# A hybrid decoder step: row values of a gated recurrence spread over partitions by transfers through DRAM, in place of matrix products

## The chip, the core and the metric

The kernel runs on one core of one Trainium2 chip, as one program. The core has a matrix engine (PE, with its weight loads shown as PEld), a vector engine (DVE), an activation engine (ACT), a general engine (POOL) and a sync engine (SP), which here issues every transfer. Each engine works through its own instructions in order; semaphores make an engine wait for another or for a transfer. The metric is the device time of one execution in microseconds, lower is better, taken as the median over runs.

## What is computed

One inference step of one layer. 16 meta tokens and 2048 prompt tokens (16 chunks of 128), and 32 sample tokens (8 sequences of 4), go through a layer norm and one input projection of width 3848. Half of the width feeds an mLSTM group (4 heads of 128, a recurrence with a running maximum), half a sliding-window attention with sinks; gates, one output projection and a second layer norm follow. The part that the change touches is the mLSTM of a chunk:

```python
b = jnp.cumsum(log_f, axis=1)
dmat = b[:, :, None, :] - b[:, None, :, :] + log_i[:, None, :, :]
inter = b + m[:, None, :]
m_t = jnp.maximum(inter, jnp.max(dmat, axis=2))
w = jnp.exp(dmat - m_t[:, :, None, :])
s_inter = jnp.exp(inter - m_t)
qk = jnp.einsum('bthd,bshd->btsh', q, k) * w
num = jnp.einsum('btsh,bshd->bthd', qk, v) + jnp.einsum('bthk,bhkv->bthv', q, c) * s_inter[..., None]
den = jnp.sum(qk, axis=2) + jnp.einsum('bthk,bhk->bth', q, n) * s_inter
h = num / jnp.maximum(jnp.abs(den), jnp.exp(-m_t))[..., None]
c_new = decay[..., None, None] * c + jnp.einsum('bsh,bshk,bshv->bhkv', w_state, k, v)
n_new = decay[..., None] * n + jnp.einsum('bsh,bshk->bhk', w_state, k)
```

The sample tokens go through the same formulas, with a state c, n, m for each of 8 sequences and 4 heads.

## The kernel before, in words

The program has a start (weights staged, scaled and split into two float16 parts, the meta and sample tokens projected) and then two long phases.

**Phase A** takes the 16 prompt chunks through the mLSTM. `a_steps(n)` is a generator whose steps are, for chunk n: the gate projection (`a_gate`), the projections q, k, v, o (`a_proj(n, 0..3)`, 24 matrix products of 128x512 each, lines 296 to 299), `m_rows(n)` (the gates are transposed so that a head is a row and time runs along it; two scans give the decay rows and the running maximum), `m_weights(n)` (the rows are brought back to one value per token and head, and the decay weights `wt` and `SI` are made), `m_S(n)` (q times k), and for the chunk before `m_num(n - 1)` and `m_kv(n - 1)`. The last two steps load x for chunk n + 2 and normalise it (`norm_x`). Between these steps a second generator, `jobs()`, is advanced: the sample tokens' mLSTM (`d_prepare`, then `d_head` for each head), the preparation of six later weights (kv, aq, az, z, o0, o1), and the sample's attention. `pace(0.8)` advances it at 8 of 10 steps.

The point that the change is about: the row M (running maximum less its own decay sum) lies on one partition per head, and the weights need it on all 128 partitions. Before, `m_weights` makes this spread with PE: `sel[:, h]` has ones in the row of head h, and four float32 products of 128x128 (line 762, two passes each) put M, spread over the partitions, in a PSUM tile from the pool `pt` (three tiles, which the transposes, the gates and the scores also use). DVE and ACT then read it there (lines 772, 776, 778). `d_prepare` does the same for the sample tokens (line 656), and in `d_head` the state C is multiplied by q in 8 products of 128 columns (line 702), each followed by one of a single column for the normaliser n (line 703).

Prepared weights are kept in a pool `wp` of five tiles. Four hold w_q, w_k, w_v, w_o through phase A; the fifth is used by one prepared weight after another, each written to DRAM (`spill`, 2 MB) before the next takes its tile, and fetched again (`reload`) when phase A leaves the tiles free.

**Phase B** takes the 16 chunks through the attention, the gates and the output projection: per chunk `b_q`, `b_kv`, `b_az`, `b_z` on PE, the score units `s_unit`, `s_pv`, and for the chunk before `b_out` (two products with wr_o, the second layer norm, the store).

A scheduler decides the order on every engine from the order of the source, the dependences and the tiles of the pools; it lets the mLSTM of a chunk run beside the projections of the next one. All transfers are issued by SP through `dma` (line 103 of the kernel before) in one order, and an issue that has to wait holds up those behind it.

## Time and profile before

| | |
|---|---|
| three runs | 1099.37, 1101.61, 1102.27 us; median 1101.61 us |
| the profiled execution | 1096.6 us, of which the span from first to last instruction is 1094.8 us |
| mean granted PE clock in it | 0.984 of full speed |
| start, until the first chunk is through its projections | about the first 110 us |
| phase A | about 110 to 560 us |
| phase B with the tail | about 560 us to the end |

A profile page gives busy times per engine, a strip of 40 slices of the span, the chain of work that ended last, and the costliest groups of instructions. Times inside the span are counted from its first instruction.

### The profile page before, as it was taken

To read this page: it belongs to the slowest core of one execution; us is meant where nothing else is said; L and a number is where in the kernel's file an instruction comes from. 1 tells how busy PE (TensorE), PEld (TensorE's weight loads), DVE (VectorE), ACT (ScalarE), POOL (GpSimd) and SP (SyncE) were. 2 spreads that over 40 slices of the span, in tenths; PEclk is the share of its full clock that TensorE was granted. 3 is DMA by queue.
4 is the path that set the end of the run, shared out by engine and by line. 5 is a ranking of instruction groups with operands and counts; after the bars stand their busy time and mean duration, and the time that the engine had idled before them with its cause. 6 is when DMAs were issued, how large, how long until landed. Compare 5 with 4: busy or idle time off the path is not lost.

```text
span 1094.8 us, 17806 instructions
## 1 busy us (share of the span) xinstructions
PE 1039.4 (95%) x6455; PEld 577.1 (53%) x6455; DVE 735.2 (67%) x2069; ACT 443.3 (40%) x1108; POOL 262.9 (24%) x270
## 2 busy tenths in 40 slices
PE   7969999999989999889998999999999999999986
PEld 3425565565556555445564554555555555555543
DVE  6769676776766777866655676566666656667664
ACT  5646333235434344562225344343344333344430
POOL 2113232121111111101311332233332233332222
PEclk9989999999999999999999999999999999999998
DMA  9746545445974568478585555656555464544552
GB/s 321 197 129 174 148 129 119 109 119 135 292 171 124 127 218 240 131 224 288 206 280 101 117 115 131 127 119 120 127 94 134 123 139 115 123 105 108 109 106 76
DMA packets 246098, 166.04 MB, mean 152 GB/s; under 512 B 207977, under 2 KB 220985, under 8 KB 244441
## 3 DMA queue, kind: packets, MB, share of 16 engines
q1 hardware_dynamic: 246010, 164.90, 58.9%
q8 instruction: 51, 0.84, 0.3%
q14 instruction: 37, 0.30, 0.1%
HBM read 70.32 MB, written 45.68 MB: 106 GB/s over the span
## 4 chain that ended last, share of the span: by engine, by line
PE 59%; DMA 15%; DVE 13%; ACT 6%; issue 5%; POOL 2%; SPq 1%; DVEq 0%; ACTq 0%; POOLq 0%
PE pj L1339 14%; PE pj L297 11%; PE pj L296 11%; PE pj L299 11%; DMA xT<-hl 3%; PE pt L1259 2%; DMA EE<-stg 2%; PE po L1312 2%; DMA stg<-in_dram 2%; DVE xs L380 1%; DMA stg<-hl 1%; DMA wd_z<-w_z 1%; DMA wd_o<-w_o 1%; ACT hl L321 1%; PE po L826 1%
## 5 line engine op out<-in xcount | busy, mean ns | idle before, releaser
L1339 PE MATMUL pj<-wr_o,EE 128*128 128x512 f16 x720 | 166.9, 381 | 3.0 <-DMA EE<-stg 1.5
L296 PEld LDWEIGHTS <-xT 128*128 128x128 f16 x992 | 97.9, 99 | 103.1 <-issue 6.9
L297 PEld LDWEIGHTS <-xT 128*128 128x128 f16 x992 | 97.8, 99 | 97.3 <-issue 6.8
L299 PEld LDWEIGHTS <-xT 128*128 128x128 f16 x992 | 96.8, 98 | 97.8
L1339 PEld LDWEIGHTS <-EE 128*128 128x128 f16 x720 | 70.5, 98 | 81.1 <-DMA EE<-stg 3.4
L325 POOL TENSOR_TENSOR lns<-lns,mhalf 128x1 f32<-128x1 f32 (+1 forms) x16 | 21.3, 1332 | 175.5 <-ACT lns L324 158.7
L1268 DVE TENSOR_TENSOR hl<-g,hl 128x512 f16<-128x512 f32 (+1 forms) x32 | 23.2, 724 | 49.1 <-ACT hl L1267 49.1
L1272 POOL TENSOR_TENSOR mhl<-g,mhl 128x32 f16<-128x32 f32 x32 | 18.8, 587 | 145.1 <-ACT mhl L1271 145.1
L296 PE MATMUL pj<-w_q,xT 128*128 128x512 f16 x120 | 47.1, 392 | 6.0 <-DMA xT<-hl 6.0
L1272 POOL TENSOR_TENSOR mhl<-SI,mhl 128x32 f16<-128x32 f32 x32 | 18.5, 578 | 139.1 <-ACT mhl L1271 139.1
L1266 ACT ACTIVATE g<-g,nb 128x272 f32<-128x272 f32 (+1 forms) x64 | 32.4, 507 | 46.3 <-DVE nb L1263 46.3
L296 PE MATMUL pj<-wr_z,xT 128*128 128x512 f16 x128 | 48.8, 381 | 0.0
L297 PE MATMUL pj<-wr_z,xT 128*128 128x512 f16 x128 | 48.7, 380 | 0.0
L296 PE MATMUL pj<-w_v,xT 128*128 128x512 f16 x120 | 46.3, 386 | 2.4 <-DVE q L431 2.4
L296 PE MATMUL pj<-wr_az,xT 128*128 128x512 f16 x128 | 48.5, 379 | 0.0
L296 PE MATMUL pj<-wr_aq,xT 128*128 128x512 f16 x128 | 48.5, 379 | 0.0
L297 PE MATMUL pj<-wr_aq,xT 128*128 128x512 f16 x128 | 48.5, 379 | 0.0
L297 PE MATMUL pj<-wr_az,xT 128*128 128x512 f16 x128 | 48.5, 379 | 0.0
L787 POOL TENSOR_TENSOR qs<-qs,SI 128x512 f32<-128x512 f32 x16 | 23.8, 1486 | 98.2 <-ACT SI L778 98.1
L297 PE MATMUL pj<-w_q,xT 128*128 128x512 f16 x120 | 47.0, 392 | 0.0
L297 PE MATMUL pj<-w_v,xT 128*128 128x512 f16 x120 | 46.5, 388 | 0.0
L297 PE MATMUL pj<-w_o,xT 128*128 128x512 f16 x120 | 46.5, 388 | 0.0
(459 smaller groups left out, 2510.4 us busy)
## 6 DMA issues: line engine op xcount, KB each, us to landing
stg<-in_dram SPq DMA_DIRECT2D x28, 512.0 KB
xs<-in_dram SPq DMA_DIRECT2D x16, 512.0 KB
h_d<-xs SPq DMA_DIRECT2D x16, 512.0 KB
xT_d<-xT SPq DMA_DIRECT2D x16, 512.0 KB
xs<-h_d SPq DMA_DIRECT2D x16, 512.0 KB
xT<-xT_d SPq DMA_DIRECT2D x16, 512.0 KB
out_dram<-xs SPq DMA_DIRECT2D x15, 512.0 KB
hn_d<-g SPq DMA_DIRECT2D x16, 258.0 KB
```

The lines of the kernel that those rows point to most:

```text
L296: T.matmul(ps, xT[:, k, :], w.t[:, k, 0, :n], start=(k == 0), stop=False)
L297: T.matmul(ps, xT[:, k, :], w.t[:, k, 1, :n], start=False, stop=False)
L299: T.matmul(ps, xT[:, KT + k, :], w.t[:, k, 0, :n], start=False, stop=(k == KT - 1))
L321: A.activation(junk[:, 0:D], x, AF.Copy, accum_out=sm)
L325: G.tensor_tensor(rs, ve, mhalf[:rows, 0:1], op=ALU.pow)
L787: G.tensor_tensor(c.qs, c.qs, c.SI, op=ALU.mult)
L1259: T.matmul(ps[:, lo:], c.qT[:, h], kTs[:, 2 * (h // 4) + x, lo:], start=(x == 0), stop=(x == 1))
L1266: A.activation(p[:, i, lo:], p[:, i, lo:], AF.Exp, bias=nb[:, h:h + 1], accum_out=sums[:, h:h + 1])
L1268: V.tensor_tensor(hl[:, 1, 2 * q:2 * q + 2, lo:], p[:, :, lo:2 * P], hl[:, 0, 2 * q:2 * q + 2, lo:], op=ALU.subtract)
L1272: G.tensor_tensor(m[:, 1], p[:, :, 2 * P:], m[:, 0], op=ALU.subtract)
L1312: T.matmul(pso[:, h], l, r, start=False, stop=(i == len(last) - 1), skip_group_check=True)
L1339: T.matmul(ps, c.yT[:, a, :], w[:, k, t, :], start=(first and j == 0), stop=(last and j == len(mm) - 1))
```

## The change

1. `sel` and its products go. `m_rows` writes each head's row of M to DRAM (four transfers of 512 bytes from one partition each) and reads the four rows back into an SBUF tile `Mb` on all 128 partitions (one transfer, 128 x 2 KB, the same 2 KB read for every partition). DVE and ACT read `Mb` there.
2. `a_gate(n + 1)` and `m_rows(n + 1)` are called in chunk n, around `a_proj(n, 3)`.
3. `d_prepare` does the same for the sample's row, with one more step of the generator.
4. In `d_head` the sample's normaliser becomes column 128 of C: 8 products of 129 columns in place of 8 of 128 and 8 of 1; the decay and the update go over 129 columns, and the separate instructions on n go; one DVE copy per head puts n in, one ACT copy takes it out.
5. x of chunk n + 3 is loaded before chunk n + 2 is normalised. The steps of a chunk are 9 instead of 10, and `pace(.92)` advances the other generator at 92 of 100 of them.
6. w_o1 is not spilled and reloaded: its tile is kept, so that the reload of aq has to wait for a tile of the projection weights. `b_out(0)` moves from chunk 1 of phase B to chunk 2, ahead of the score units.

The core of the diff:

```diff
-    sel = cst.tile([P, H, P], F32, name="sel")
-    G.memset(sel, 0.0)
-    for h in range(H):
-        G.memset(sel[32 * h:32 * h + 1, h], 1.0)
...
+    m_d = [dr.tile([H, P], F32, name=f"m_d{n}") for n in range(NCH)]
+    m5_d = dr.tile([H, 40], F32, name="m5_d")
...
-        ps = pt([P, H, 40])
         for h in range(H):
-            T.matmul(ps[:, h], sel[:, h], M5, start=True, stop=True)
-        A.activation(Mb5.rearrange("p h b s -> p (h b s)"), ps.rearrange("p h t -> p (h t)"), AF.Copy)
+            dma(m5_d[h:h + 1], M5[32 * h:32 * h + 1])
+        dma(Mb5.rearrange("p h b s -> p (h b s)"), m5_d.rearrange("(o h) t -> o (h t)", o=1).partition_broadcast(P))
+        yield
...
-        dma(C3, st_c[:, h].rearrange("b k v -> k b v"))
+        C3 = C.rearrange("p (b d) -> p b d", d=129)
+        dma(C3[:, :, 0:P], st_c[:, h].rearrange("b k v -> k b v"))
+        V.tensor_copy(C3[:, :, P], E.nS.rearrange("p (b h) -> p h b", h=H)[:, h])
...
-            T.matmul(ps[:NS, :128], z, C3[:, b], start=False, stop=False, skip_group_check=True)
-            T.matmul(ps[:NS, 128:129], z, E.nS[:, b * H + h:b * H + h + 1], start=False, stop=(b == 7),
-                     skip_group_check=True)
+            T.matmul(ps[:NS, :129], z, C3[:, b], start=False, stop=(b == 7), skip_group_check=True)
...
-        c.r2, c.M = r2, M
+        for h in range(H):
+            dma(m_d[n][h:h + 1], M[32 * h:32 * h + 1])
+        c.Mb = work("Mb", [P, H, P])
+        dma(c.Mb.rearrange("p h t -> p (h t)"), m_d[n].rearrange("(o h) t -> o (h t)", o=1).partition_broadcast(P))
+        c.r2 = r2
...
-        Mb = pt([P, H, P])
-        for h in range(H):
-            T.matmul(Mb[:, h], sel[:, h], c.M, start=True, stop=True)
+        Mb = c.Mb
...
-        spill(w, f"o{i}")
+        if i == 0:
+            spill(w, "o0")
...
+            if n + 1 < NCH:
+                ca[n + 1] = St()
+                ca[n + 1].xT = xTs.pop(n + 1)
+                a_gate(n + 1)
             if n > 0:
                 a_proj(n, 3)
+            if n + 1 < NCH:
+                m_rows(n + 1)
             m_S(n)
...
-            if pace(0.8):
+            if pace(.92):
...
-    for nm in ("az", "z", "o0", "o1"):
+    for nm in ("az", "z", "o0"):
...
+        if n == 2:
+            b_out(0)
```

How the order of instructions moves, at three places.

PE late in phase A, before: the end of the k projection of chunk 15 (line 297), then the spread of M of chunk 14 (line 762), the transposes of its rows (line 765), and the first of the scores (line 797).

```order
L297 MATMUL pj<-w_k,xT 128x512
L762 MATMUL pt<-rM,sel 128x128 x4
L765 MATMUL pt<-cs,r_5176 128x128 x2
L797 LDWEIGHTS kT
L797 MATMUL pt<-qT,kT 128x128
```

The same transposes in the changed kernel (there line 762 is the transpose; lines 807 and 808 are the two products of `m_num`, 509 is the gate of the next chunk):

```order
L297 MATMUL pj<-w_o,xT 128x512
L807 MATMUL po<-vaug_118,At 128x129
L808 MATMUL po<-Cst_683,qs 128x129
...
L762 MATMUL pt<-cs,r_5078 128x128 x2
L509 LDWEIGHTS xT
L509 MATMUL pt<-w_g,xT 128x16
```

The four spreading products are gone, and the transposes no longer stand directly ahead of the scores.

SP in phase A of the changed kernel, around the spill of the prepared az weight (2 MB); `m_d10` are the four rows of chunk 10, `Mb` their spread, and the transposes qT and kT and the store hn_d9 belong to chunks 10 and 9:

```order
L103 DMA m_d10_186<-rM_3834 1x128 x4
...
L103 DMA ea_3683<-in_7_dram 48x512
L103 DMA stg_3654<-in_4_dram 128x1024
L103 DMA wd_az_3671<-w_az_3343 128x8192
L103 DMA Mb_3843<-m_d10_186 128x512
L103 DMA_TRANSPOSE qT_3908<-qh_3905 128x8x128
L103 DMA hn_d9_168<-g_3911 128x516
L103 DMA_TRANSPOSE kT_3966<-kh_3963 128x8x128
```

The rows and their spread are new in SP's order; here the spread stands directly behind a 2 MB spill and ahead of both transposes of its chunk.

SP at the end of phase A, before (the names: `wd_` is the copy of a weight in DRAM, `wr_` its tile when fetched again, qT and kT are those of chunks 14 and 15):

```order
L103 DMA wr_aq_5079<-wd_aq_2810 128x8192
L103 DMA wr_kv_5081<-wd_kv_2253 128x4096
...
L103 DMA_TRANSPOSE qT_5150<-qh_5147 128x8x128
L103 DMA_TRANSPOSE kT_5212<-kh_5209 128x8x128
...
L103 DMA wr_az_5605<-wd_az_3733 128x8192
...
L103 DMA_TRANSPOSE qT_5394<-qh_5391 128x8x128
L103 DMA wr_z_5607<-wd_z_4211 128x8192
...
L103 DMA_TRANSPOSE kT_5456<-kh_5453 128x8x128
...
L103 DMA wr_o0_5609<-wd_o0_4672 128x8192
...
L103 DMA wr_o1_5611<-wd_o1_5040 128x8192
```

and in the changed kernel:

```order
L103 DMA wr_kv_4971<-wd_kv_2230 128x4096
...
L103 DMA_TRANSPOSE qT_5150<-qh_5147 128x8x128
L103 DMA_TRANSPOSE kT_5200<-kh_5197 128x8x128
...
L103 DMA wr_aq_4969<-wd_aq_2729 128x8192
...
L103 DMA_TRANSPOSE qT_5395<-qh_5392 128x8x128
...
L103 DMA m_d15_191<-rM_5339 1x128 x4
L103 DMA_TRANSPOSE kT_5445<-kh_5442 128x8x128
L103 DMA Mb_5348<-m_d15_191 128x512
...
L103 DMA wr_az_5589<-wd_az_3671 128x8192
L103 DMA wr_z_5591<-wd_z_4065 128x8192
...
L103 DMA wr_o0_5593<-wd_o0_4568 128x8192
```

Each reload has moved back: aq now stands where az stood, az and z follow the last spread, and o1 has gone.

## The prediction

> **What bounds the kernel now.** I read the page's busy times first, then its strip of slices and the chain that ended last, then the windows that cut the span into its stages, and last the list of what PE waited for.

> ```profile
> PE 1039.4 (95%) x6455; PEld 577.1 (53%) x6455; DVE 735.2 (67%) x2069; ACT 443.3 (40%) x1108; POOL 262.9 (24%) x270
> PE   7969999999989999889998999999999999999986
> PEclk9989999999999999999999999999999999999998
> PE 59%; DMA 15%; DVE 13%; ACT 6%; issue 5%; POOL 2%; SPq 1%; DVEq 0%; ACTq 0%; POOLq 0%
> ...
> core 0: us, PE busy (x) PEld busy (x) DVE busy (x) ACT busy (x) POOL busy (x), PEclk, DMA share, GB/s
> 0.00:110.00 110.00, 91.16 (x371) 45.59 (x372) 81.80 (x223) 63.86 (x114) 21.30 (x31) 0.95 0.71 206
> 110.00:560.00 450.00, 430.27 (x2716) 250.97 (x2714) 314.77 (x905) 179.03 (x402) 81.46 (x63) 0.99 0.63 178
> 560.00:610.00 50.00, 46.05 (x282) 26.35 (x280) 30.97 (x113) 21.66 (x69) 8.79 (x18) 0.97 0.62 141
> 610.00:1060.00 450.00, 448.08 (x2953) 242.42 (x2951) 291.40 (x801) 174.46 (x512) 144.83 (x153) 1.00 0.54 117
> ```

> PE is busy 95% of the span. In phase A (110 to 560 us) it is busy 430.27 of 450 us, in the steady part of phase B 448.08 of 450. DVE, the next, has 314.77 of 450 in phase A, so it has 135 us to spare. Nearly all that the change touches lies in phase A. There PE's own work sets the time; 19.7 us of waits are spread over it. A matrix product taken from PE in phase A shortens the kernel by its own spacing, unless its successor (a transfer, or a DVE instruction that waits for it) comes too late.

> **What leaves PE.** The spread of M, the sample's spread, and the one-column products, in PE's timeline (start, length, line, operation, tiles, count; a float32 product counts as two):

> ```profile
> 344.10 1.05 PE L762 MATMUL pt<-rM,sel 128*128 128x128 f32 x8
> 344.99 0.38 PE L765 MATMUL pt<-cs,r 128*128 128x128 f32 x2
> ...
> 94.58 0.98 PE L656 MATMUL pt<-ea,sel 128*128 128x40 f32 x8
> 95.39 0.39 PE L299 MATMUL pj<-w_v,xT 128*128 128x512 f16 x1
> ...
> 219.71 0.38 PE L702 MATMUL px<-da 128*32 128x128 f32 x2
> 219.93 0.20 PE L703 MATMUL px<-ea,da 128*32 128x1 f32 x2
> 219.99 0.38 PE L702 MATMUL px<-da 128*32 128x128 f32 x2
> ```

> Products overlap in their last part, so I take the distance from one start to the next group's start. M's spread: 344.99 - 344.10 = 0.89 us, 16 chunks, **14.2 us**. The sample's: 95.39 - 94.58 = **0.8 us**, once. In `d_head` a sequence takes 219.99 - 219.71 = 0.28 us, of which the products of 128 columns take 219.93 - 219.71 = 0.22; one column more does not show at this resolution. 0.06 us, 8 sequences, 4 heads: **1.9 us**. Together 16.9 us.

> **The waits that go with it.** M's spread held one of the three `pt` tiles until ACT had made SI from it.

> ```profile
> PE pt L135 <- ACT SI L778: 2.9, 1, 2.9
> PE pt L511 <- ACT am L767: 1.1, 2, 0.8
> PE pt L511 <- ACT SI L778: 0.4, 1, 0.4
> PE px L728 <- DVE ea L707: 3.3, 3, 1.6
> ```

> The two waits for ACT's SI (line 778) are waits for that tile: PE could not start a product into `pt`. SI now reads SBUF, so these 2.9 + 0.4 = **3.3 us** go. The wait for `am` is for the transposes' tile, which stays, and so does the 3.3 us of `px`, since that pool of one tile is untouched. Bounds: 0, where another holder of `pt` is late next, to 4.4 with `am`. I take 3.3, from the rows that name SI.

> **What is added: five transfers a chunk, and a wait.** No row shows a row of 512 bytes written to DRAM and read back by all partitions. The nearest, from the chain of waits and from SP's timeline:

> ```profile
> 205.86 2.30 DMA da<-e_d
> ...
> 534.62 9.09 DMA bias<-in_dram
> ...
> 423.26 12.16 DMA wd_z<-w_z
> ...
> 552.55 1.16 SPq L103 DMA_DIRECT2D out_dram<-r  x4
> 463.37 10.45 SPq L103 DMA_TRANSPOSE xT<-hl  x1
> ```

> A 64 KB read from DRAM landed 2.30 us after its issue with little beside it. A read of the very shape of `Mb` (one row of 512 read by 128 partitions, a bias) took 9.09 us in the full queue at the end of phase A. Four stores from one partition of r cost SP 1.16 us to issue. So rows and spread take between 2 x 2.30 = 4.6 us and 2 x 9.09 = 18.2 us. What lies over them is a chunk:

> ```profile
> 400.01 0.27 PE L743 MATMUL pt<-cs,Gf 128*128 128x128 f32 x1
> 432.16 0.27 PE L743 MATMUL pt<-cs,Gf 128*128 128x128 f32 x1
> ```

> Line 743 opens `m_rows`, once a chunk: 32.15 us apart. Since M is made while the chunk before is still at its projections, most of that is cover, and I cost the latency itself at **0**. If the cover were gone, it would cost at least 4.6 x 16 = 74 us. SP pays 1.16 + about 0.4 us of issue and the landing of the rows (2.30 or more) per chunk, some 4 us in 32; behind it stand qT, kT and hn_d, whose users come most of a chunk later.

> The danger is the big spills. While wd_o was going out, SP sat 10.45 us on one transpose, and wd_z took 12.16 us. Rows or a spread behind them can be up to 12.16 + 9.09 us late, and DVE, in order, stops at the first reader of `Mb` (line 769 of the changed kernel); behind that stand the evictions of the projections, and PE has two `pj` tiles. Such a stop already stands in the trace, by another road: ACT waited 4.46 us for wd_z, and the eviction of q came late:

> ```profile
> 435.49 1.06 ACT L257 ACTIVATE w_o<-stg 128x1024 f16<-128x1024 f32 x1 [4.46 <-DMA wd_z<-w_z]
> ...
> 442.50 0.58 PE L296 MATMUL pj<-w_v,xT 128*128 128x512 f16 x1 [2.41 <-DVE q L431]
> 442.88 0.63 PE L297 MATMUL pj<-w_v,xT 128*128 128x512 f16 x1
> 443.31 0.63 PE L296 MATMUL pj<-w_v,xT 128*128 128x512 f16 x1
> ...
> 440.00:460.00 20.00, 16.46 (x105) 10.13 (x104) 17.04 (x38) 13.59 (x28) 3.27 (x3) 0.91 0.46 115
> ```

> PE idled 2.41 us, and behind the gap the products start 0.43 us apart: the granted clock is 0.91 over these 20 us, another 20 x 0.09 = 1.8 us. One such stop costs 4.2 us. I allow **one new one, 4.2 us**. Bounds: 0, and four (after aq, az, z and o0) at 9.09 + 1.8 each, 43.6 us.

> [...]

> **What is moved, and the rest at nothing.** The transfers taken away (o1 out and in, 2 MB each) were on no PE wait. No wait of PE names `wr_o`; 0, with the 4.2 us of one stop as the bound on the good side. The reload of aq loses its lead, as it must wait for w_q's tile:

> ```profile
> L103 SPq DMA_DIRECT2D wr_aq<-wd_aq x1: 320/320/320, 506.4 to 506.4; - x1
> ...
> 531.86 0.38 PE L299 MATMUL pj<-w_q,xT 128*128 128x512 f16 x1
> L296 PE MATMUL pj<-wr_aq,xT x128: 379/379/380, 553.1 to 1027.9; 128*128 128x512 f16 x128
> ```

> It was issued 46.7 us before use. Now it can start at 532.2, when the last q product is through, with 20.9 us to 553.1; 2 MB took 12.16 us. 0, and if it also sits behind a 9.09 us queue, 0.4. `am`, `wt` and SI do the same work from SBUF. The earlier x, the denser pace and the moved `b_out` change no amount of PE work, and no PE wait names x; 0, up to one stop either way. The DVE and ACT copies in `d_head` replace four small DVE instructions per head.

> **The sum.** -16.9 - 3.3 + 4.2 = **-16.0 us**. Of the profiled execution's 1096.6 us that leaves 1080.6. The three runs have a median of 1101.61, 5.0 us above the profiled one, and the same work leaves them too: 1101.6 - 16.0 = **1085.6 us**.

> **Rivals.**

> *No new stop, and an old one gone.* The transposes no longer follow a spread, `pt` is freer, and late evictions like that at 442.50 fall away with it: -16.9 - 3.3 - 4.2 - 1.8 = -26.2, or 1075.4 us. For it: three of the four waits of PE quoted above name ACT. Against it: ACT still waits for the same spills.

> *The gain is lost in waits.* PE's products go, but phase A is paced by the chain of DVE, ACT and SP beside it, and PE only idles more: about -2 to 0, or 1101 us. For it: PE, DMA, DVE and ACT all stand in the chain that ended last (59, 15, 13 and 6%). Against it: PE is busy 95.6% of phase A and DVE 70%.

> *Spread late behind the spills.* In all four places a spread lands after DVE has come to it, and PE stops for 9.09 us and pays 1.8 us of clock: 43.6 - 20.2 = +23.4, or 1125 us. It decides where rows and spread together land later than the time from line 743 to line 769's turn on DVE, at most one chunk of 32.15 us; a spill (12.16) and two loaded transfers (18.2) make 30.4, so it is near but needs every place at its worst.

> *The change does not do what it says*: a spread that is not early, where the scheduler keeps the old place of `m_rows`. SP's order shows rows and spread ahead of the chunk's own transposes, so I give this no chance of its own; it would end as the third rival.

> **How the numbers follow.** Forecast 0.70, old stop gone 0.12, lost in waits 0.10, spread late 0.08. The forecast's own range is 1079 to 1093 (no new stop, to two more). To leave out no more than 2 in 10, the whole range goes from 1071 (below the second case) to 1102 (with the third case). About 0.3%, 3.3 us, is what a measurement of this kernel tells from no change. Faster by more: the first two cases, 0.82. Within: 0.10. Slower by more: 0.08.

> **What would show it.** PE's busy time near 1039.4 - 17 = 1022 us, with no product from `sel`. Phase A shorter by 14 to 20 us, phase B unchanged per chunk. No wait of PE on `pt` for SI. Waits of DVE at `ws` or `wt` on a transfer `Mb` only behind a spill. The forecast is wrong if PE's idle time in phase A grows by more than a few us beyond 19.7, if DVE's longest waits name `Mb`, or if PE waits for wr_aq, wr_az or wr_z at the start of phase B.

## The result, and the profile after

The changed kernel takes 1088.18 us (median of four runs, 1085.34 to 1092.41) against 1101.15 us for the kernel before in the same session (four runs, 1099.37 to 1102.27). The ratio is 0.9887, with a 95% interval of 0.9851 to 0.9923: 13.0 us faster (8.5 to 16.4 by the interval), where 16.0 us were forecast. The total came out; several of its terms did not. They erred both ways, and that the errors cancelled so nearly is in part luck. The experiments show which terms.

The page after: busy times, the strips for PE and its granted clock, and the shares of the chain that ended last.

```profile
span 1085.8 us, 17483 instructions
PE 1025.6 (94%) x6255; PEld 559.8 (52%) x6255; DVE 748.4 (69%) x2057; ACT 446.3 (41%) x1111; POOL 258.6 (24%) x265
PE   6977998999999999989999999999999999999986
PEclk9997999999999999999999999999999999999998
PE 62%; DMA 14%; DVE 13%; issue 4%; ACT 3%; SPq 2%; POOL 1%; DVEq 0%; ACTq 0%; POOLq 0%
```

PE has 13.8 us less work (1039.4 before), but its share of the span fell from 95 to 94%: PE idles 60.2 us, 4.8 more than before. The profiled pair differs by 9.0 us of span, the medians by 13.0. The profiled run of before, 1096.6 us, is faster than each of the 47 other runs of that kernel in this study (the fastest of them 1097.75), so a sum made on it starts 5 us too low.

From the list of what PE waited for, after (total, times, longest):

```profile
PE po L640 <- DVE gts L515: 5.3, 1, 5.3
PE po L1318 <- DMA stg<-hl: 4.9, 3, 1.8
PE po L823 <- DVE Cst L824: 4.7, 4, 2.6
...
PE pj L294 <- DVE q L429: 2.7, 2, 1.5
```

The waits for ACT's SI are gone. New is the first line shown, in the start. PE's timeline and two windows there:

```profile
92.98 0.59 PE L297 MATMUL pj<-w_v,xT 128*128 128x512 f16 x2
98.82 0.55 PE L640 MATMUL po<-vaug,kw 16*128 16x129 f32 x1 [5.25 <-DVE gts L515]
...
92.00:99.00 7.00, 1.75 (x24) 1.08 (x23) 7.00 (x15) 3.71 (x9) 7.00 (x4) 0.81 0.68 195
98.80:106.80 8.00, 7.98 (x23) 3.97 (x24) 5.37 (x22) 3.21 (x9) 0.34 (x1) 0.52 0.77 260
```

DVE is busy for all 7.00 us of the first window: here it is the bound, and the sample's spread and the scores that stood here before had lain over its work. Taking them out left a hole of 5.25 us, and behind it the granted clock is 0.52 for 8 us. The kernels of the table below bear this out: the wait ahead of this product is 0.2 to 2.1 us in the four that still spread with PE (before, e1, e3, e4) and 3.7 to 6.9 us in the ten that spread by transfers, also in e2, where no reader of a chunk waits for `Mb`.

How far ahead the rows are: M written by DVE, its transfers on SP and the first readers, chunk 15.

```profile
535.66 0.35 DVE L748 SCALAR_TENSOR_TENSOR rM<-r,r,rb 128x128 f32<-128x128 f32 x1
...
536.14 1.13 SPq L103 DMA_DIRECT2D m_d<-rM  x4
538.24 1.24 SPq L103 DMA_TRANSPOSE kT<-kh  x1
539.67 0.45 SPq L103 DMA_DIRECT2D Mb<-m_d  x1
...
542.96 0.17 DVE L769 TENSOR_TENSOR ws<-am,Mb 128x4 f32<-128x4 f32 x1 [0.43 <-DMA Mb<-m_d]
542.95 0.63 ACT L775 ACTIVATE SI<-Mb 128x512 f32<-128x512 f32 x1 [1.06 <-DMA Mb<-m_d]
```

From the end of `rM` to SI are 6.9 us here; over the 16 chunks 5.1 to 26.6 us, median 8.4. That is far from a chunk. In most chunks a reader waits for the transfer:

```profile
DVE ws L769 <- DMA Mb<-m_d: 17.6, 9, 5.1
...
ACT SI L775 <- DMA Mb<-m_d: 29.2, 13, 4.8
```

### The profile page after: what moved, and what is told of

It reads as the page before. It is cut to its first block, busy times and chain, and to the rows that moved or that the text cites. A ratio compares the mean times of both kernels' runs of the same rounds, so it can differ in the third digit from the quotient of the medians.

```text
span 1085.8 us, 17483 instructions
## 1 busy us (share of the span) xinstructions
PE 1025.6 (94%) x6255; PEld 559.8 (52%) x6255; DVE 748.4 (69%) x2057; ACT 446.3 (41%) x1111; POOL 258.6 (24%) x265
## 4 chain that ended last, share of the span: by engine, by line
PE 62%; DMA 14%; DVE 13%; issue 4%; ACT 3%; SPq 2%; POOL 1%; DVEq 0%; ACTq 0%; POOLq 0%
PE pj L1345 13%; PE pj L294 12%; PE pj L295 12%; PE pj L297 12%; DMA xT<-hl 4%; DMA Mb<-m_d 3%; DMA stg<-hl 2%; PE pt L1265 2%; PE po L1318 2%; SPq L103 2%; DVE wt L773 1%; DMA xs<-in_dram 1%; DMA stg<-in_dram 1%; DVE xs L378 1%; DVE xs L377 1%
## 5 line engine op out<-in xcount | busy, mean ns | idle before, releaser
L295 PEld LDWEIGHTS <-xT 128*128 128x128 f16 x992 | 97.6, 98 | 103.3 <-issue 11.1
L297 PEld LDWEIGHTS <-xT 128*128 128x128 f16 x992 | 96.3, 98 | 95.8 <-issue 1.4
L1345 PE MATMUL pj<-wr_o,EE 128*128 128x512 f16 x360 | 87.3, 379 | 0.2
L1345 PE MATMUL pj<-w_o,EE 128*128 128x512 f16 x360 | 82.5, 386 | 0.2 <-DVE qs L1232 0.2
L783 POOL TENSOR_TENSOR qs<-qT 128x512 f32<-128x512 f16 x16 | 23.0, 1436 | 149.9 <-DMA qT<-qh 81.2
L1278 POOL TENSOR_TENSOR mhl<-g,mhl 128x32 f16<-128x32 f32 x32 | 19.6, 612 | 134.7 <-ACT mhl L1277 129.7
L294 PE MATMUL pj<-w_k,xT 128*128 128x512 f16 x120 | 45.8, 381 | 2.7 <-DVE q L429 2.7
```

Source lines behind the costliest of these rows:

```text
L294: T.matmul(ps, xT[:, k, :], w.t[:, k, 0, :n], start=(k == 0), stop=False)
L295: T.matmul(ps, xT[:, k, :], w.t[:, k, 1, :n], start=False, stop=False)
L297: T.matmul(ps, xT[:, KT + k, :], w.t[:, k, 0, :n], start=False, stop=(k == KT - 1))
L783: G.tensor_tensor(c.qs, c.qT[:, 0], c.qT[:, 1], op=ALU.add)
L1278: G.tensor_tensor(m[:, 1], p[:, :, 2 * P:], m[:, 0], op=ALU.subtract)
L1345: T.matmul(ps, c.yT[:, a, :], w[:, k, t, :], start=(first and j == 0), stop=(last and j == len(mm) - 1))
```

## The experiments

Two theories to begin with. **Theory 1**, the prediction's: phase A is PE's own work, each product taken out is worth its spacing, and some is given back where DVE and ACT wait for `Mb`. **Rival 2**: the spread is worth little, and the other parts of the change made the gain. After the first four kernels came **theory 4**: PE has stops in phase A into which products fit for nothing; what an edit is worth depends on which stops the order gets, and each longer stop costs its idle time and some clock on top (1.8 us behind the stop of 2.41 us at 442.50 in the kernel before).

All are read against the kernel before, run beside them. The profile gives each run's span and mean granted clock. I split the time with them: span times clock is my estimate of what the run would have taken at full clock ("full-speed part"), the rest is counted as lost to the clock. Both are means over the runs. The last column cuts the profiled run at the first and the last product that line 294 (296 before) makes with the reloaded aq weight: start and phase A, phase B, tail.

The changed kernel itself was timed once, four runs in an earlier session, in which the kernel before had a median of 1101.15 us; in the three later sessions it had 1103.24 to 1104.97. So a difference to the changed kernel depends on how it is taken. The third column gives both: by the medians, and by the ratios to the kernel before (times 1101). They lie 1.6 to 5.0 us apart, and the interval of the changed kernel's ratio alone is 4 us to either side. A difference to it is called clear only where both readings bear it out.

| kernel | median us | to the changed kernel, us: by medians, by ratios | ratio, 95% interval | PE busy | full-speed part + lost | parts of the profiled run |
|---|---|---|---|---|---|---|
| before | 1103.84, 1104.97, 1103.24 in three sessions |  | 1 | 1039.4 | 1082.3 + 19.6 | 553.1, 474.8, 66.9 |
| changed | 1088.18 |  | 0.9887 (0.9851 to 0.9923) | 1025.6 | 1069.7 + 17.1 | 548.8, 468.5, 68.5 |
| e1, spread on PE again | 1094.23 | +6.0, +3.0 | 0.9914 (0.9886 to 0.9943) | 1037.4 | 1077.6 + 14.8 | 556.2, 468.8, 65.6 |
| e2, nobody waits for Mb | 1086.39 | -1.8, -5.4 | 0.9838 (0.9815 to 0.9861) | 1023.9 | 1063.9 + 20.4 | 542.7, 472.6, 67.3 |
| e3, before + merged column | 1095.09 |  | 0.9926 (0.9899 to 0.9953) | 1035.9 | 1079.4 + 14.6 | 554.6, 472.3, 65.2 |
| e4, before + spread twice | 1101.39 |  | 0.9977 (0.9961 to 0.9993) | 1051.0 | 1086.5 + 13.0 | 564.4, 473.7, 63.0 |
| e5, before + transfers, not ahead | 1134.19 | +46.0, +41.0 | 1.0259 (1.0235 to 1.0283) | 1035.9 | 1090.9 + 40.7 | 563.2, 497.3, 67.3 |
| e11, rows earlier | 1085.35 | -2.8, -7.3 | 0.9821 (0.9800 to 0.9843) | 1022.8 | 1064.1 + 19.1 | 549.2, 470.5, 62.7 |
| e12, column not merged | 1099.23 | +11.1, +6.8 | 0.9949 (0.9932 to 0.9966) | 1028.3 | 1076.6 + 20.7 | 560.3, 469.7, 67.5 |
| e7, old x and old pace | 1081.15 | -7.0, -10.0 | 0.9796 (0.9772 to 0.9819) | 1020.7 | 1062.9 + 17.5 | 547.8, 467.1, 62.6 |
| e13, old pace alone | 1095.64 | +7.5, +5.5 | 0.9937 (0.9915 to 0.9960) | 1025.0 | 1069.5 + 24.4 | 547.8, 481.6, 62.6 |
| e17, 32 columns more | 1095.92 | +7.7, +5.9 | 0.9941 (0.9921 to 0.9961) | 1026.3 | 1072.9 + 21.5 | 558.6, 468.2, 66.8 |
| e15, e7 + rows in one transfer | 1098.74 | +10.6, +7.7 | 0.9957 (0.9937 to 0.9978) | 1030.3 | 1071.3 + 25.7 | 554.9, 472.0, 65.5 |
| e16, e15 + rows earlier | 1082.21 | -6.0, -7.6 | 0.9818 (0.9794 to 0.9843) | 1020.1 | 1064.1 + 16.6 | 549.2, 466.9, 64.3 |

### The spread on PE again

The main part of the edit; the sample's spread in `d_prepare` goes back to PE in the same way.

```diff
-        Mb = c.Mb
+        Mb = pt([P, H, P])
+        for h in range(H):
+            T.matmul(Mb[:, h], sel[:, h], c.M, start=True, stop=True)
```

> The changed kernel with the spread made by PE again (16 x 4 products with sel, and the sample's 4), all else of the change kept, the rows one call ahead too. Theory 1 (the products that left PE are the gain, some of it given back where DVE and ACT wait for Mb): PE does 14.2 + 0.8 us more, the waits for the transfer Mb (46.8 us before DVE and ACT) go; against the changed kernel +8 to +13 us, so about 1096 to 1101 us and a ratio to the kernel before of 0.995 to 1.000. Rival 2 (the spread is worth little, the earlier x, the denser pace, the kept o1 and the merged column made the 13 us): 0 to +4 us against the changed kernel, ratio 0.988 to 0.992.

Measured: 6.0 us slower than the changed kernel by the medians, which is between the theories; 3.0 us by the ratios, which is rival 2's range, and the two intervals overlap. PE's busy time rose by 11.8 us, the full-speed part by 7.9, and less clock was lost. The transfers in place of the products are worth some 3 to 6 us, not the 8 to 13 of theory 1. Whether it is within rival 2's 0 to 4 us or somewhat more, this run does not decide.

### Nobody waits for the spread

```diff
-        c.Mb = work("Mb", [P, H, P])
-        dma(c.Mb.rearrange("p h t -> p (h t)"), m_d[n].rearrange("(o h) t -> o (h t)", o=1).partition_broadcast(P))
+        Mb = work("Mb", [P, H, P])
+        c.Mb = bA[0].rearrange("p (h t) -> p h t", t=P)
+        dma(Mb.rearrange("p h t -> p (h t)"), m_d[n].rearrange("(o h) t -> o (h t)", o=1).partition_broadcast(P))
```

> The changed kernel in which every transfer of rows and spread is still issued, but DVE and ACT read another tile that has long been there (a bias) in place of Mb: the mLSTM's weights are computed from other numbers, and what is left out is the wait. Theory 1 (the late spread costs PE late evictions): 3 to 6 us faster than the changed kernel, about 1082 to 1085 us, and the short waits of PE for Cst, At, q and k (13 us in all) shrink by that. Rival 3 (DVE and ACT have slack, so the 46.8 us of waits for Mb are free): within 1.5 us of the changed kernel.

Measured: 1.8 us faster than the changed kernel by the medians, short of the 3 us of theory 1; 5.4 us by the ratios, within its 3 to 6; the intervals of the two ratios overlap. The full-speed part is 5.8 us lower, 3.3 us of it lost again to the clock. Whether the late spread costs 2 or 5 us stays open; either way the 46.8 us that DVE and ACT wait for `Mb` reach the time only in small part. The edit leaves the sample's spread as it is, and the scheduler could place the readers elsewhere.

### The merged column alone

The edit takes the change's `d_head` into the kernel before.

> The kernel before with the sample's normaliser as a column of C alone. Theory 1 (PE work is the time): 32 one-column products less, 1.9 us faster than before, ratio 0.998. Rival: the sample's products stand in a chain with one px tile that DVE and POOL pace, so nothing, ratio 1.000; the added copies cost at most 0.5 us.

Measured: 8.7 us faster than the kernel before in the same session, over four times the 1.9 us of theory 1; the rival had nothing, so both miss. PE's busy time fell by 3.5 us, the full-speed part by 2.9, and 5.0 us less was lost to the clock.

### The spread twice

```diff
             T.matmul(Mb[:, h], sel[:, h], c.M, start=True, stop=True)
+            T.matmul(Mb[:, h], sel[:, h], c.M, start=True, stop=True)
```

> The kernel before with each of the 64 products that spread M made twice into the same tile. Theory 1 (phase A is PE's own work): +14.2 us at 0.89 us a chunk, ratio 1.013. Rival 2 (the spread lay in time in which PE would have waited anyway): +3 to +7 us, ratio 1.003 to 1.006.

Measured: 0.2% *faster* than the kernel before, with 11.6 us more work on PE. Both theories miss. The page and the window of phase A:

```profile
span 1101.1 us, 18041 instructions
PE 1051.0 (95%) x6583; PEld 589.0 (53%) x6583; DVE 728.2 (66%) x2069; ACT 441.9 (40%) x1108; POOL 259.7 (24%) x270
...
110.00:560.00 450.00, 434.02 (x2772) 256.91 (x2771) 311.35 (x901) 175.24 (x390) 79.90 (x62) 0.99 0.61 171
```

PE idles 50.1 us over the span (55.4 before). By the table 4.2 us of the 14.2 us show in the full-speed part, and 6.6 us less is lost to the clock. The two profiled runs alone would have said otherwise: 6.3 us longer, and 11.3 us longer to the end of phase A. But the profiled run of before is 7.2 us faster than the median of the 17 runs of before beside e4, and the medians are those of 12 and 17 runs. PE work in phase A is therefore not the time one for one.

### Not ahead

The kernel before with `m_rows` and `d_prepare` as the change has them, called where they were before.

> The kernel before with the spread of M and of the sample's row made by transfers through DRAM, but nothing called ahead: rows, then one projection, then their use. Theory 1 as the prediction has it (a chunk of cover is what hides the latency; without it at least 4.6 us a chunk): 74 us slower than the changed kernel, above 1160 us. Theory 4 (even in the changed kernel the rows stand only about 8 us ahead of their use, DVE has some 30% to spare, and PE works on other chunks meanwhile): 2 to 8 us slower than the changed kernel, 1090 to 1096 us, ratio 0.988 to 0.994, with DVE and ACT waiting some 80 to 120 us for Mb instead of 46.8.

Measured: 46.0 us slower than the changed kernel by the medians (41.0 by the ratios), 29 slower than before. Theory 4's small price is refuted, and the 74 us too large. Readers wait longer, and PE stops:

```profile
ACT SI L778 <- DMA Mb<-m_d: 48.4, 16, 9.0
DVE ws L772 <- DMA Mb<-m_d: 38.3, 14, 7.5
...
PE pj L1339 <- DMA EE<-stg: 12.5, 3, 10.3
PE pt L1259 <- DMA o<-k: 7.5, 1, 7.5
PE px L726 <- DVE ea L705: 7.2, 4, 3.7
```

Against the profiled run of before, 10.1 us are lost by the end of phase A and 22.5 in phase B, where the first two PE lines stand. Why those transfers were late there was not tried. Against the kernel before, transfers that are not ahead lose 29 us; in the changed kernel, ahead, they gain 3 to 6 (e1). That the call ahead makes this difference is likely but not isolated: the two pairs also differ in x, pace, column, o1 and `b_out`.

### Rows earlier

The lines added; the same calls go from behind `m_T` and the fourth projection.

```diff
             m_weights(n)
+            if n + 1 < NCH:
+                ca[n + 1] = St()
+                ca[n + 1].xT = xTs.pop(n + 1)
+                a_gate(n + 1)
+                m_rows(n + 1)
             yield
```

> The changed kernel with the gate and the rows of chunk n + 1 called directly behind the weights of chunk n, two projections and m_kv earlier. Theory 4: the waits for Mb fall from 46.8 us to under 15, and the time by what the run without the wait gave, 2 to 4 us against the changed kernel, about 1084 to 1086 us, ratio 0.982 to 0.986. Rival 5 (the earlier gate makes PE wait for xT of the next chunk, or new stops appear elsewhere): 0 to +6 us against the changed kernel.

Measured: 2.8 us faster than the changed kernel by the medians (7.3 by the ratios), so faster as expected, but not for the reason given: the waits for `Mb` stayed at 43.4 us. The intervals of the two ratios lie just apart (0.9843 and 0.9851).

### The column not merged, and 32 columns more

The first has the `d_head` of before in the changed kernel. The second adds, behind each of the 32 merged products, one of a single column. Its added products begin sums of their own in the tile, and the sample tokens' y is not that of the changed kernel, so it serves for the time alone.

```diff
             T.matmul(ps[:NS, :129], z, C3[:, b], start=False, stop=(b == 7), skip_group_check=True)
+            T.matmul(ps[:NS, 136:137], z, C3[:, b, P:129], start=True, stop=True, skip_group_check=True)
```

> The changed kernel with the sample's normaliser as products of one column again, as before. Theory 1 (work alone): +1.9 us against the changed kernel. Theory 4 (which stops there are decides, as when the merged column alone made the kernel before 8 us faster at a higher granted clock): the full-speed part (span times granted clock) rises by 1.9 to 3.5 us, the part lost to the clock can go either way by 5 us, so -3 to +8 us.

> The changed kernel (normaliser merged) with 32 products of one column more, each with the weights of the product ahead of it and into columns of the same tile that nobody reads. Theory 1 (their work): +1.9 us against the changed kernel, 1088.5 to 1091.5 us, ratio 0.988 to 0.991. If such a product itself is dear (a load of 32 weights for one column, and the wait for it): +8 to +11 us, as undoing the merge gave. If undoing the merge moved stops elsewhere: below +4 us.

Measured: 11.1 and 7.7 us slower than the changed kernel by the medians (6.8 and 5.9 by the ratios), at 2.7 and 0.7 us more PE busy time. The first is far above theory 1's 1.9; theory 4 had at most 8 us, which the medians miss and the ratios do not, and 1.9 to 3.5 us in the full-speed part, which rose by 6.9. The second lies between its two answers. In the profiled runs the spans are 11.7 and 7.8 us longer, and 9.0 and 7.1 us of that are idle time of PE (69.2 and 67.3 us against 60.2). Where the time stands is seen in PE's timeline at one place, the first o product of a chunk late in phase A: the changed kernel, with the 10 us from one microsecond ahead of it,

```profile
479.24 0.38 PE L294 MATMUL pj<-w_o,xT 128*128 128x512 f16 x1 [1.76 <-DVE k L429]
...
478.20:488.20 10.00, 8.96 (x53) 4.72 (x53) 5.45 (x19) 1.82 (x3) 0.00 (x0) 1.00 0.18 33
```

the one with the column not merged,

```profile
488.77 0.38 PE L294 MATMUL pj<-w_o,xT 128*128 128x512 f16 x1 [4.01 <-DVE k L429]
...
487.80:497.80 10.00, 9.03 (x45) 4.45 (x45) 4.05 (x12) 1.10 (x2) 0.00 (x0) 0.83 0.00 0
```

and the one with 32 columns more:

```profile
487.46 0.58 PE L294 MATMUL pj<-w_o,xT 128*128 128x512 f16 x1 [2.60 <-DVE k L429]
...
486.50:496.50 10.00, 9.04 (x45) 4.41 (x45) 4.06 (x12) 1.11 (x2) 0.00 (x0) 0.83 0.00 1
```

The same stop is 1.76 us with no clock lost, or 4.01 or 2.60 us with 10 x 0.17 = 1.7 us lost. In the trace without the merge the stop for `da` in `d_head` is longer too, 4.81 us at 186.66 (2.32 at 180.85 in the changed kernel). Most of the price is in stops, not in the products. What lengthens them I could not isolate.

### x and pace

```diff
-            if pace(.92):
+            if pace(0.8):
```

The first kernel also loads x two chunks ahead, as before; the second has this edit alone.

> The changed kernel with x loaded two chunks ahead as before and the second generator advanced at 8 of 10 steps. Rival 2 (these made part of the gain): 3 to 8 us slower than the changed kernel. Theory 1 (they are worth nothing): within 1.5 us of the changed kernel, ratio 0.985 to 0.990.

> The changed kernel with the second generator advanced at 8 of 10 steps as before, x still three chunks ahead. Undoing pace and x together gave 7 us against the changed kernel. If the pace alone does it: 1079 to 1084 us, ratio 0.977 to 0.982. If the early x does it: within 1.5 us of the changed kernel. Theory 4 (any such edit moves the scheduler's order and with it the stops, by a few us up or down, each stop its idle time and about 1.8 us of clock): anything from -6 to +6 us, at the same amount of PE work within 1 us.

Measured: both undone, 7.0 us faster than the changed kernel by the medians (10.0 by the ratios), where rival 2 had 3 to 8 us slower and theory 1 nothing: both miss. Pace alone undone, 7.5 us slower (5.5 by the ratios): neither single cause holds, and theory 4's -6 to +6 holds by the ratios only. In the second, one new wait is as large as the whole difference and more, in PE's timeline and the 20 us around it:

```profile
566.93 0.37 PE L294 MATMUL pj<-wr_kv,xT 128*128 128x256 f16 x1 [9.85 <-DMA wr_kv<-wd_kv]
...
560.00:580.00 20.00, 13.07 (x61) 7.15 (x61) 8.74 (x30) 4.42 (x12) 8.35 (x8) 0.70 0.66 170
```

The reload of kv was issued at 556.0 us, 503.1 in the changed kernel. The stop costs 9.85 us and 20 x 0.30 = 6.0 us of clock. By an estimate from these two, the kernel without it would be at 1095.6 - 15.9 = 1079.8 us, about level with e7; that was not run. So the edit is not priced by its own content. The early x alone was not tried.

### The rows in one transfer, and with the earlier call

```diff
-        for h in range(H):
-            dma(m_d[n][h:h + 1], M[32 * h:32 * h + 1])
+        dma(m_d[n], M[0:P:32])
```

> The changed kernel with x and pace as before (which gave 1081.2 us) and the four rows of M written by one transfer from four partitions in place of four transfers. SP issues 48 transfers less, at about 0.3 us each 0.9 us a chunk. Theory 4: the waits for Mb fall from 41.6 us to about 28 and the time by 1 to 3 us, 1078 to 1080 us, ratio 0.976 to 0.978. Rival: the latency of rows and spread is in the two landings and not in the issue, 0 to -1 us.

> The same with the gate and the rows of chunk n + 1 called directly behind the weights of chunk n. Called early in the changed kernel they gave 3 us, though the waits for Mb stayed at 43.5 us. If the gains add: 1076 to 1079 us, ratio 0.973 to 0.976. If each only moved stops: 1079 to 1085 us.

Measured: 17.6 us slower than the kernel it was made from (e7), and with the earlier call 1.1 us slower than e7, where the intervals of the two ratios overlap. No theory had the first; the second is in the range for "each only moved stops". The waits for `Mb` grew to 55.4 us, and of PE's stops in phase A this one shows how such a loss is made up. In e7, with its window:

```profile
147.53 0.28 PE L688 MATMUL px<-cs,da 32*128 32x32 f32 x2 [1.49 <-DMA da<-e_d]
...
146.50:156.50 10.00, 8.97 (x71) 6.28 (x71) 7.18 (x17) 2.76 (x9) 4.58 (x4) 1.00 0.97 202
```

and with one transfer for the rows:

```profile
152.14 0.39 PE L688 MATMUL px<-cs,da 32*128 32x32 f32 x2 [3.55 <-DMA da<-e_d]
...
151.10:161.10 10.00, 8.96 (x45) 4.40 (x46) 7.76 (x30) 3.14 (x11) 4.39 (x3) 0.66 0.89 215
```

2.1 us of idle time more, and 3.4 us of clock that were not lost before. Of the 17.6 us, by the table, 8.4 are full-speed part and 8.2 clock. By the median the fastest version remains e7, faster than both kernels: its interval (0.9772 to 0.9819) lies below that of the changed kernel. From e16 and e11 its interval does not separate it.

## Why the prediction was right, and where not

**The total.** 1085.6 us forecast, 1088.2 measured. The direction and the size were right by a sum whose terms erred both ways, so the closeness of the total is partly luck.

**PE's work, -16.9.** PE's busy time fell by 13.8 us, and no product with `sel` is left. The step that failed is "A matrix product taken from PE in phase A shortens the kernel by its own spacing": the spread (15.0 with the sample's) is worth 3 to 6 us (e1), the same products made a second time cost 4.2 us of full-speed time and no time at all in the end (e4), and in the start the products taken out left a stop of 5.25 us. The other way, the one-column products (1.9) were worth 8.7 us alone and 11.1 us in the changed kernel by the medians, 6.8 by the ratios (e3, e12).

**The waits for SI, -3.3.** They are gone, as forecast.

**One new stop, +4.2.** Neither the place nor the cause was right: nothing behind a spill, but the stop in the start. Its size was over twice that: 5.25 us of idle time and 8 x 0.48 = 3.8 us of clock. What late spreads cost in all is 1.8 us by the medians, 5.4 by the ratios (e2).

**The latency at 0.** "most of that is cover" failed: the rows stand 8.4 us ahead of their use at the median, not most of 32.15, and 22 of the readers' waits name `Mb` (46.8 us). I took the distance between two `m_rows` for the distance from rows to use, and only the second counts. The cost was small nevertheless, since DVE has time to spare (329.51 us busy of the 450 of phase A). The price without cover (at least 74 us) was too high; it measured 41 to 46 against the changed kernel (e5), in a kernel that differs in more than the cover.

**The rest at nothing.** "phase B unchanged per chunk" held where phase B is steady: from the first aq product of a chunk to that of the next are 32.2 us for most chunks from the fourth on, in both kernels. Phase B as cut in the table went from 474.8 to 468.5 us in the profiled pair, and 4.9 of these 6.3 us lie between the first aq products of chunks 0 and 3 (93.9 and 89.0 us). A part of that is phase A's work on the other side of the cut: the kernel before spreads M of chunk 15, and makes its scores, behind the first aq product.

```profile
553.11 0.38 PE L296 MATMUL pj<-wr_aq,xT 128*128 128x512 f16 x1
...
554.41 1.05 PE L762 MATMUL pt<-rM,sel 128*128 128x128 f32 x8
```

In the changed kernel the last scores are done at the first aq product. How much of the rest is the moved `b_out` and the kept o1 was not tried. x and pace together cost 7.0 us by the medians, 10.0 by the ratios (e7). No PE wait names wr_aq, wr_az or wr_z, as forecast; that the reloads are hidden holds for this order only (e13).

**The signs named beforehand.** The idle time of PE in phase A grew by only 1.8 us (450 less 428.45 busy, against 19.7), but DVE's fourth longest wait names `Mb`, and the readers wait for it in most chunks and not only behind a spill. By that second sign the forecast would have been called wrong, and it was not: the sum of these waits is no measure of the time.

```profile
110.00:560.00 450.00, 428.45 (x2626) 244.57 (x2624) 329.51 (x901) 183.84 (x410) 79.91 (x65) 0.99 0.63 181
```

"Phase A shorter by 14 to 20 us" failed. Up to the first aq product, before and after:

```profile
0.00:553.10 553.10, 514.54 (x3037) 292.10 (x3038) 393.00 (x1117) 238.98 (x504) 101.49 (x93) 0.98 0.64 181
0.00:548.80 548.80, 504.67 (x2864) 278.22 (x2865) 405.55 (x1112) 245.02 (x515) 99.19 (x89) 0.98 0.63 182
```

That is 4.3 us. PE is busy 9.9 us less and idles 5.6 us more: over half of what left PE here came back as stops. The medians differ by 4.0 us more than these two spans; even if all of that belonged to this part, it would be 8.3 us.

**The working.** Three slips of it do not touch the forecast. The first rival takes 1.8 us of clock off a second time, as the 4.2 us hold it: 1077.2 us, not 1075.4. The forecast's own range, from no new stop to two more, is 1081.4 to 1094.0 by its terms, not 1079 to 1093. And where it says that no PE wait names x, PE's longest wait in the kernel before, 6.0 us in the start, is for xT, which is made from x.

**What stays open**: how much of each part's worth is the part itself, and how much the order that the scheduler happened to make. Kernels within 10.2 us of each other in PE's busy time (e7, e11, e13, e15, e16 and the changed one) spread over 17.6 us.

## What to carry to other kernels

Where the bound engine has many short stops, the work taken from it is no price: the spread gave back less than its work (3 to 6 us of 15.0), the merged column more. Split measured runs into full-speed part and clock loss, and look at the list of stops before and after. For data made ahead, measure from its making to its first reader, not from one making to the next. And price an edit of a scheduled kernel in more than one surrounding (do it alone, undo it alone): here the same merge gave 7 to 11 us where its work was 1.9, and one transfer for the rows in place of four cost 17.6 us in one kernel, while the kernel that also calls the rows earlier stood within 1.1 us of where that one began. And time two kernels that are to be compared in one session: here the kernel before moved by up to 3.8 us between sessions, as much as several of the differences.

## What the runs showed of the hardware

**A mean clock that differs between programs.** Runs of the kernel before had 0.978 to 0.987, those of e4 0.986 to 0.990, those of e15 0.974 to 0.981. One hundredth of mean clock is 11 us of this span, nearly as much as the whole change.

**Small transfers through DRAM.** From M in SBUF to its first reader behind two dependent transfers: 5.1 us at the least, median 8.4 (the changed kernel's 16 chunks; in some of them the reader itself came later than the transfer).
